# Feed-forward pair combinations on VectorE, early products, and side work moved into the mLSTM stage of a two-layer trunk

## The chip, the cores and the metric

The kernel is one program on one core of a Trainium2 chip. The metric is the device time of one execution in microseconds (us); the kernel before took 3206.36 us as the median of three runs (3194.96 to 3218.95).

## What is computed

The reference is a trunk of two layers over 1024 tokens of width 1024, in float32. Each layer has a token mixer (RWKV-7 in layer 0, a chunked mLSTM in layer 1) and a SwiGLU feed-forward block, each behind an RMS norm whose scale, shift and gate come from the conditioning vector `c` (`mod`):

```python
mod = c_act @ ada_w[i] + ada_b[i]
sh1, sc1, g1, sh2, sc2, g2 = split(mod, 6)
x = x + g1 * mixer(_rms(x) * (1 + sc1) + sh1)      # _rwkv7_mix (i = 0) or _mlstm_mix (i = 1)
x = x + g2 * _swiglu(_rms(x) * (1 + sc2) + sh2, w_gu, w_down)
...
def _swiglu(x, w_gu, w_down):
    gu = x @ w_gu
    return (silu(gu[..., :D_FF]) * gu[..., D_FF:]) @ w_down      # D_FF = 2816
```

After layer 1 a last RMS norm is scaled by `final_w`.

## The kernel before

Activations lie transposed: 8 tiles of 128 features by 512 tokens for each of two token halves (`x[0]`, `x[1]`). A float32 product is made of three reduced-precision ones: `split` (L210) makes a rounded part `hi` on ScalarE and the rest `lo = raw - hi` on VectorE, and for every 128x128 block of weights TensorE runs hi*hi, hi*lo and lo*hi, each a matmul of 128x512.

The feed-forward (`ffn`, L1053) uses a Winograd form of Strassen's scheme over both token halves: instead of 8 block products of half size, `seven` (L902) runs 7 for a pair of output tiles n and n+11, from seven combinations of weight blocks (`wpair`, L863) and seven of activations (`X`). A block product is 4 blocks x 3 = 12 matmuls, so a call of `seven` is 84. There are 11 pairs, each with a call for the gate and one for the up projection. The first two pairs (`NPLAIN`) are done without the scheme: `plain`, 48 matmuls for each of two tiles and two halves, 192 for a pair instead of 168. `wpair` loads two weight tiles, and makes the four sums and differences on GpSimd (L881 to L888, into `ws`), between splits of 512 columns. `keep` stores each pair's results and their own combinations to DRAM (`gd`), and `down` (L987) reads them back for the second matrix, again in seven products, with combinations of its weights that `sums` (L966) wrote to DRAM before (`wsd`).

`sums` and `ada` (layer 1's `mod`, L289) are background work: generators in `self.bg`, of which `wpair` advances `rate` steps each time. A step of `sums` loads four tiles of 128x352, makes four sums on GpSimd and stores four; there are 16 for each layer. `ada` loads 512-column tiles and accumulates on VectorE; a 1-column matmul ends each. In layer 0 the rate is 7, with `sums(0)` and then all six parts of `ada`; in layer 1 it is 1, with `sums(1)`. The mLSTM stage has no background work.

All these transfers are issued by SP's queue, in order: an issue that waits for a buffer holds up those behind it. A scheduler lays the instructions of each engine in one fixed order, and `ahead(...)` raises the priority of some. Buffers are pools by tag (`FROOM` for the feed-forward: 4 `tmp`, 8 `tt`, 3 `wraw`; 8 `x` for activations and later the background).

The RWKV stage (`chunks`, L1386) works through 16 units (8 feature tiles x 2 halves) in a pipeline of preparation, inverse, solve, chain and finish; `fillers` puts dense matmuls between their small, dependent ones, and its last filler is the output projection of token half 0. The projection of half 1 (`second`) comes in `ffn`, after the plain tiles of half 0.

## Time and profile before

| | before |
|---|---|
| median of 3 runs | 3206.36 us (3194.96 to 3218.95) |
| profiled execution, its own time | 3216.39 us |
| span of its trace | 3214.2 us |
| TensorE busy (matmul) | 2946.6 us, 92% |
| VectorE / ScalarE / GpSimd busy | 1950.4 / 1437.8 / 428.8 us |
| granted TensorE clock, mean | 0.905 |

The stages, by what TensorE's matmuls read: layer 0's inputs and RWKV to about 1120 us, feed-forward of layer 0 to about 1943, mLSTM to about 2380, projection and feed-forward of layer 1 to the end. A granted clock of 1.00 is 2.4 GHz, 0.50 is 1.2 GHz. Matmuls overlap their neighbours in the pipeline, so the count of matmuls in a stretch tells more than the duration of one.

### The profile page before, as it was taken

The page shows a single profiled execution, that of the slowest core. Times are in us where ns is not written, and L with a number is a line of the kernel's source. Part 1 is how long each engine was busy: PE and PEld are TensorE (multiplying, and loading weights), DVE is VectorE, ACT ScalarE, POOL GpSimd, SP SyncE. Part 2 cuts the span into 40 slices and gives each one's busy share as a digit, 9 for nine tenths or more (in the row PEclk, how much of TensorE's full clock was granted, in tenths as well). Part 3 has the DMA queues.
Part 4 walks back from the last instruction along what each step waited for, and adds up shares of the span by engine and source line. Part 5 has one row for each costly group of instructions (what it writes and reads, how often), then busy time and mean ns, then how long its engine had stood idle before and what let it go on. Part 6 is the DMA issues. An engine that isn't in the chain of part 4 may idle for free. (4 is left out here: it accounts for less than half of the span.)

```text
span 3214.2 us, 46353 instructions
## 1 busy us (share of the span) xinstructions
PE 2946.6 (92%) x16960; PEld 2318.8 (72%) x16960; DVE 1950.4 (61%) x3736; ACT 1437.8 (45%) x2815; POOL 428.8 (13%) x369
## 2 busy tenths in 40 slices
PE   6899999999999888958899999999988898899997
PEld 5577667777776676747788887777767776688886
DVE  7867576777665447638957656434455564555763
ACT  5656665655654444312335436333334432333551
POOL 0000000000000001652220000000000066431000
PEclk9899688899788598978999999898988899999998
DMA  8764343344533243666737643111144256533852
GB/s 290 266 214 126 94 129 98 104 113 132 152 111 107 66 140 108 207 226 214 236 122 252 215 165 108 33 40 40 46 164 136 97 180 213 184 105 129 288 170 89
DMA packets 318679, 474.78 MB, mean 148 GB/s; under 512 B 120652, under 2 KB 163276, under 8 KB 318452
## 3 DMA queue, kind: packets, MB, share of 16 engines
q1 hardware_dynamic: 304628, 446.66, 43.7%
q10 hardware_dynamic: 13824, 25.17, 2.1%
q8 instruction: 133, 2.18, 0.3%
q14 instruction: 94, 0.77, 0.1%
HBM read 347.98 MB, written 123.73 MB: 147 GB/s over the span
## 5 line engine op out<-in xcount | busy, mean ns | idle before, releaser
L208 PE MATMUL c<-ga,wq 128*128 128x512 f32 x1998 | 490.3, 400 | 53.2 <-ACT tmp L911 32.5
L212 ACT ACTIVATE wq<-wraw 128x512 fp32r<-128x512 f32 (+2 forms) x368 | 248.3, 678 | 584.1 <-PE c L208 265.4
L208 PEld LDWEIGHTS c<-ga,wq 128*128 128x128 f32 x1998 | 382.5, 193 | 142.6 <-ACT tmp L911 37.3
L213 DVE TENSOR_TENSOR wq<-wraw,wq 128x512 fp32r<-128x512 f32 (+2 forms) x368 | 304.6, 833 | 283.7 <-ACT wq L212 280.0
L208 PE MATMUL dn<-a,whi 128*128 128x512 f32 (+2 forms) x1048 | 401.9, 449 | 17.4 <-ACT a L212 6.2
L208 PEld LDWEIGHTS dn<-a,whi 128*128 128x128 f32 (+2 forms) x1048 | 206.1, 204 | 77.9 <-issue 11.5
L208 PE MATMUL c<-gb,wq 128*128 128x512 f32 x1014 | 248.0, 398 | 4.5 <-DVE tt L926 2.3
L208 PE MATMUL dn<-a,wlo 128*128 128x512 f32 (+2 forms) x552 | 244.0, 446 | 7.1 <-ACT tmp L416 2.2
L208 PE MATMUL dn<-ga,wq 128*128 128x512 f32 x894 | 224.3, 400 | 14.9 <-ACT ga L212 11.1
L208 PEld LDWEIGHTS c<-gb,wq 128*128 128x128 f32 x1014 | 192.9, 192 | 49.1 <-DVE tt L926 3.9
L208 PEld LDWEIGHTS dn<-ga,wq 128*128 128x128 f32 x894 | 173.3, 195 | 54.2 <-ACT ga L212 12.1
L213 DVE TENSOR_TENSOR wlo<-wraw,whi 128x1024 fp32r<-128x1024 f32 (+2 forms) x86 | 103.9, 1208 | 142.3 <-ACT whi L212 137.2
L212 ACT ACTIVATE wq<-ws 128x512 fp32r<-128x512 f32 x108 | 67.4, 629 | 221.6 <-POOL ws L882 97.1
L208 PE MATMUL px<-ga,wq 128*128 128x512 f32 x552 | 141.1, 411 | 27.1 <-ACT tmp L911 20.0
L208 PE MATMUL iv<-gb,wq 128*128 128x512 f32 x630 | 151.4, 390 | 0.0
L213 DVE TENSOR_TENSOR wq<-ws,wq 128x512 fp32r<-128x512 f32 x108 | 84.3, 782 | 105.4 <-ACT wq L212 104.5
L208 PEld LDWEIGHTS px<-ga,wq 128*128 128x128 f32 x552 | 109.5, 200 | 53.0 <-ACT tmp L911 21.8
L208 PE MATMUL dn<-gb,wq 128*128 128x512 f32 x522 | 127.9, 398 | 17.9 <-ACT gb L212 10.0
L208 PEld LDWEIGHTS dn<-a,wlo 128*128 128x128 f32 (+2 forms) x552 | 113.9, 207 | 35.9 <-issue 5.7
L212 ACT ACTIVATE whi<-wraw 128x1024 fp32r<-128x1024 f32 (+2 forms) x86 | 89.7, 1044 | 105.8 <-PE dn L208 91.5
L208 PEld LDWEIGHTS iv<-gb,wq 128*128 128x128 f32 x630 | 118.2, 188 | 24.5
L208 PEld LDWEIGHTS dn<-gb,wq 128*128 128x128 f32 x522 | 99.5, 191 | 41.2 <-ACT gb L212 10.3
(547 smaller groups left out, 5562.7 us busy)
## 6 DMA issues: line engine op xcount, KB each, us to landing
wraw<-in_wgu SPq DMA_DIRECT2D x104, 512.0 KB, 3.7
tt<-gd SPq DMA_DIRECT2D x154, 256.0 KB, 4.7
x<-in_ada SPq DMA_DIRECT2D x96, 256.0 KB, 3.8
gd<-tt SPq DMA_DIRECT2D x88, 256.0 KB, 3.1
x<-in_wdn SPq DMA_DIRECT2D x128, 176.0 KB, 3.3
wsd<-x SPq DMA_DIRECT2D x128, 176.0 KB, 1.8
KT<-in_ada SPq DMA_DIRECT2D x40, 512.0 KB, 5.7
gd<-tmp SPq DMA_DIRECT2D x66, 256.0 KB, 3.7
```

The source lines that it names most:

```text
L208: return self.nc.tensor.matmul(out, lhsT, rhs, start=start, stop=stop, **kw)
L212: self.nc.scalar.activation(hi, src, AF.Copy)
L213: self.nc.vector.tensor_tensor(lo, src, hi.bitcast(F32), SUB)
```

## The change

- Weight combinations: `wpair` makes the four sums and differences in place in the two loaded tiles, on VectorE, and splits them in pieces of 1024, 512, 1024 and 1024 columns instead of seven of 512. `down` splits 1024 columns at once as well.
- Pairs: no pair is plain. For eight pairs of layer 0 (0 to 7) and three of layer 1 (0 to 2), `first` runs products 1 and 2 ahead (their operands are blocks of token half 0 alone), stores product 1 to `pd` and the finished first result to `gd`. When their turn comes ("there"), `seven` runs the five other products (60 matmuls) and adds product 1 from `pd` on VectorE, at the two places where ScalarE copied before.
- Where they run: five of layer 0's as the last fillers of the RWKV stage, behind the projection of half 0 and its norm; the other three, and layer 1's three, in `ffn` between the steps that prepare `X`. `second` now comes first in `ffn`. In the loop the pairs with all seven products come first.
- Background: `sums` works on VectorE, in steps of up to 256 columns (24 for a layer), `ada` in tiles of 256 columns; both in one single buffer of four parts (`bgs`, or `st` in the mLSTM stage), so that a step's loads wait until the buffer's last user is done. Layer 0's feed-forward keeps `sums(0)` and three parts of `ada`, at two steps for each `wpair` and one for each weight tile of `down`; the other three parts and `sums(1)` go to the mLSTM stage, at three steps for each weight tile. Layer 1's feed-forward has none.
- The last norm takes the tiles that are finished first ahead of the others.

```diff
-NPLAIN = 2
+EARLY = ((0, 5, 8), (0, 0, 3))
...
-FROOM = {"wraw": (3, 1024), "wq": (8, 1024), "gb": (11, 1024), "ws": (3, 512), "tmp": (4, 512), "ga": (17, 1024),
-         "tt": (8, 512), "rs": (1, 4)}
+FROOM = {"wraw": (3, 1024), "wq": (5, 2048), "w4": (2, 1024), "gb": (11, 1024), "bgs": (1, 1024), "tt": (5, 512),
+         "ga": (17, 1024), "rs": (1, 4)}
...
-    def ada(self, s, w, raw, acc):
...
+    def spare(self):
+
+        return self.t("bgs" if "bgs" in self.pools else "st", [P, 4, 256])
+
+    def ada(self, s):
...
         for f in range(0, D, w):
-            t = self.t(acc, [P, w])
+            room = self.spare()
+            t = room[:, 0]
             for kt in range(KT):
-                m = self.t(self.alt(*raw), [P, w])
+                m = room[:, 1 + kt % 3]
...
-                if kt < KT - 1:
+                if kt % 2 and kt < KT - 1:
                     yield
...
+    def wpair(self, s1, s2, most):
 
...
-        def part(n, src):
-            out[n] = self.two("wq")
-            self.split(*out[n], src)
-        with self.ahead("pair"):
-            r1, r2 = (self.t("wraw", [P, D]) for _ in range(2))
-            nc.sync.dma_start(r1, s1)
-            nc.sync.dma_start(r2, s2)
-            a11, a12, a21, a22 = r1[:, :HT], r1[:, HT:], r2[:, :HT], r2[:, HT:]
-            u, v, w = (self.t("ws") for _ in range(3))
-            add = nc.gpsimd.tensor_tensor
-            part(1, a11)
-            part(2, a12)
-            add(u, a21, a22, ADD)
-            add(v, u, a11, SUB)
-            part(6, v)
-            part(5, u)
-            add(a21, a11, a21, SUB)
-            part(7, a21)
-            part(4, a22)
-            add(w, a12, v, SUB)
-            part(3, w)
+        def parts(ns, src):
+            n = len(ns)
+            q = self.t("wq" if n == 2 else "w4", [P, 2, n * HT], F32R)
+            self.split(q[:, 0], q[:, 1], src)
+            for i, m in enumerate(ns):
+                c = slice(i * HT, i * HT + HT)
+                out[m] = q[:, 0, c], q[:, 1, c]
+        r1, r2 = (self.t("wraw", [P, D]) for _ in range(2))
+        nc.sync.dma_start(r1, s1)
+        nc.sync.dma_start(r2, s2)
+        a11, a12, a21, a22 = r1[:, :HT], r1[:, HT:], r2[:, :HT], r2[:, HT:]
+        if most:
+            parts((1, 2), r1)
+        parts((4,), a22)
+        add = nc.vector.tensor_tensor
+        add(a22, a21, a22, ADD)
+        add(a21, a11, a21, SUB)
+        add(a11, a22, a11, SUB)
+        add(a12, a12, a11, SUB)
+        parts((6, 3), r1)
+        parts((7, 5), r2)
...
-    def seven(self, w, X, tag):
+    def seven(self, w, X, tag, p1=None):
...
-        def copy(ps):
+        def take(ps):
             t = self.t(tag)
-            nc.scalar.activation(t, ps, AF.Copy)
+            if p1 is None:
+                nc.scalar.activation(t, ps, AF.Copy)
+            else:
+                nc.vector.tensor_tensor(t, ps, p1, ADD)
             return t
...
+        c11 = None
+        if p1 is None:
+            self.product(a, w[1], X[1])
+            c11 = take(a)
+            b = other()
+            self.product(b, w[2], X[2])
+            nc.vector.tensor_tensor(c11, b, c11, ADD)
+        self.product(a, w[6], X[6], start=p1 is not None)
+        c12 = take(a)
...
-        c21 = copy(a)
+        c21 = take(a)
...
+    def first(self, l, n, hp, tags):
+
+        nc = self.nc
+        out = []
+        for u in range(2):
+            hi, lo = self.weights(self.A["wgu"][l, NF * u + n])
+            pa, pb = (self.bank("dn") for _ in range(2))
+            self.product(pa, (hi[:, :HT], lo[:, :HT]), hp[:4])
+            p1 = self.t(tags[0])
+            nc.scalar.activation(p1, pa, AF.Copy)
+            nc.sync.dma_start(self.pd[u, n], p1)
+            self.product(pb, (hi[:, HT:], lo[:, HT:]), hp[4:])
+            t = self.t(tags[1])
+            nc.vector.tensor_tensor(t, pb, p1, ADD)
+            out.append(t)
+        g, u = out
+        nc.scalar.activation(g, g, AF.Silu)
+        nc.vector.tensor_tensor(g, u, g, MUL)
+        nc.sync.dma_start(self.gd[0, n], g)
...
-        q = k // 4
-        add = nc.gpsimd.tensor_tensor
+        add = nc.vector.tensor_tensor
         for n in range(4):
-            for c in range(0, k, q):
-                a11, a21, a22, a12 = (self.t("x", [P, q]) for _ in range(4))
+            for c in range(0, k, 256):
+                q = min(256, k - c)
+                room = self.spare()
+                a11, a21, a22, a12 = (room[:, i, :q] for i in range(4))
                 for t, m, o in ((a11, n, 0), (a21, n + 4, 0), (a22, n + 4, k), (a12, n, k)):
                     nc.sync.dma_start(t, w[l, m, :, o + c:o + c + q])
-                s1, s2 = (self.t("x", [P, q]) for _ in range(2))
-                add(s1, a21, a22, ADD)
-                add(s2, s1, a11, SUB)
+                add(a22, a21, a22, ADD)
                 add(a21, a11, a21, SUB)
-                add(a12, a12, s2, SUB)
-                for i, t in enumerate((s1, s2, a21, a12)):
-                    nc.sync.dma_start(self.wsd[i, n, :, c:c + q], t)
+                add(a11, a22, a11, SUB)
+                add(a12, a12, a11, SUB)
+                for i, t in enumerate((a22, a11, a21, a12)):
+                    nc.sync.dma_start(self.wsd[l][i, n, :, c:c + q], t)
                 yield
...
+        _, n0, n1 = EARLY[l]
+        if l == 1:
+            self.store(0, x[0])
+            r = self.rstd(x[0])
+        second()
+        if l == 1:
+            self.norm_blocks(x[0], l, r)
         b11, b21 = self.parts(x[0][:4], "gb"), self.parts(x[0][4:], "gb")
...
+        with self.ahead("norm"):
+            r = self.rstd(x[1])
+        tags = "tt", "tt"
+
+        def some():
+            nonlocal n0
+            if n0 < n1:
+                self.first(l, n0, b11 + b21, tags)
+                n0 += 1
+        some()
+        X = {1: b11, 2: b21}
+        f = [x[0][:4], x[1][:4], x[0][4:], x[1][4:]]
...
+        X[3], X[6] = [], []
         for kt in range(4):
-            f11, f21, f12, f22 = x[0][kt], x[0][kt + 4], x[1][kt], x[1][kt + 4]
-            nc.vector.tensor_tensor(f12, f12, f11, SUB)
-            nc.vector.tensor_tensor(f22, f22, f12, SUB)
-            nc.vector.tensor_tensor(f21, f21, f22, SUB)
...
+            self.norm_blocks(x[1], l, r, (kt, kt + 4))
+            add(f[1][kt], f[1][kt], f[0][kt], SUB)
+            X[3] += self.parts(f[3][kt:kt + 1], "gb" if kt < 3 else "ga")
+            add(f[3][kt], f[3][kt], f[1][kt], SUB)
+            X[6] += self.parts(f[3][kt:kt + 1], "ga")
+        some()
+        X[5] = self.parts(f[1], "ga")
+        X[7] = []
+        for kt in range(4):
+            add(f[0][kt], f[3][kt], f[0][kt], SUB)
+            X[7] += self.parts(f[0][kt:kt + 1], "ga")
+        some()
+        X[4] = []
+        for kt in range(4):
+            add(f[2][kt], f[2][kt], f[3][kt], SUB)
+            X[4] += self.parts(f[2][kt:kt + 1], "ga")
+        while n0 < n1:
+            some()
+        self.rate = rates[0]
+        for n in chain(range(n1, NH), range(n1)):
+            there = n < n1
+            w = wgu[l]
+            p = [None] * 2
+            if there:
+                p = [self.t("tt") for _ in range(2)]
+                nc.sync.dma_start(p[0], self.pd[0, n])
+            sil = self.seven(self.wpair(w[n], w[n + NH], not there), X, "x", p[0])
+            if there:
+                sil[0] = self.t("x")
+                nc.sync.dma_start(sil[0], self.gd[0, n])
+            for t in sil[there:]:
                 nc.scalar.activation(t, t, AF.Silu)
-            up = self.seven(self.wpair(wgu[l, NF + n], wgu[l, NF + n + NH]), X, "tmp")
-            for t, u in zip(sil, up):
+            if there:
+                nc.sync.dma_start(p[1], self.pd[1, n])
+            up = self.seven(self.wpair(w[NF + n], w[NF + n + NH], not there), X, "tt", p[1])
+            for t, u in zip(sil[there:], up[there:]):
                 nc.vector.tensor_tensor(t, u, t, MUL)
-            self.keep(sil, n, up[:3])
-        self.background(1000)
-        self.rate = 0
+            self.keep(sil, n, up[there:][:3], there)
+        self.rate = rates[1]
         x[0] = self.load(self.rooms(0), 0, self.xd[0])
         x[1] = self.load(self.rooms(1), 1, self.xd[1])
         self.down(l, x, done)
+        self.background(1000)
+        self.rate = 0
...
-        r = self.rstd(xs)
+        r = self.rstd(xs[4:] + xs[:4] if hf else xs)
...
         yield from self.project(self.yd[0], "wro", 0, x0, self.a0, PA)
+        self.store(0, x0)
+        self.norm_blocks(x0, 0, self.rstd(x0))
+        hp = []
+        for x in x0:
+            hi, lo = self.a0()
+            self.split(hi, lo, x)
+            hp.append((hi, lo))
+        for n in range(EARLY[0][0], EARLY[0][1]):
+            self.first(0, n, hp, ("mt", "tmp"))
+            yield 11
...
+        self.deep = True
+
+        def second(y, w, l):
             x[1] = self.load(self.rooms(1), 1, None if l == 0 else self.xd[1])
-            run(self.project(y, w, l, x[1], lambda: self.two("ga"), tag))
-        self.bg = chain(self.sums(0), *(self.ada(s, HT, RAW1, "x") for s in (1, 0, 2, 4, 3, 5)))
-        self.ffn(0, x, lambda: second(self.yd[1], "wro", 0, ("tmp",)), lambda j: self.store(j, x[j]), 7)
+            run(self.project(y, w, l, x[1], lambda: self.two("ga"), ("tt",)))
+        self.bg = chain(self.sums(0), *(self.ada(s) for s in (1, 0, 2)))
+        self.ffn(0, x, lambda: second(self.yd[1], "wro", 0), lambda j: self.store(j, x[j]), (2, 1))
...
         self.deep = True
+        self.bg, self.rate = chain(*(self.ada(s) for s in (4, 3, 5)), self.sums(1)), 3
...
         run(ml)
+        self.background(1000)
+        self.rate = 0
...
+        run(self.project(self.yd[0], "wmo", 1, x[0], lambda: self.two("gb"), ("tt",)))
+        self.ffn(1, x, lambda: second(self.yd[1], "wmo", 1), lambda j: self.final(j, x[j]), (0, 0))
```

TensorE near the end of the RWKV stage, in the last unit's chain; `st` is the state, `AR`, `KT`, `SR` and `VU` are the unit's operands, `a` the split activations of token half 0. Before:

```order
L208 MATMUL c_2071_11335<-VU_11188,KT_10616 128x128
L208 MATMUL c_2070_11332<-VU_11188,SR_10571 64x64 x2
L208 MATMUL c_2072_11342<-st_1580,AR_10559 128x128
L208 MATMUL c_2073_11345<-VU_11188,KT_10616 128x128
L208 MATMUL c_2072_11342<-VU_11188,SR_10571 64x64 x2
L208 MATMUL c_2074_11352<-st_1580,AR_10559 128x128
```

Now:

```order
L207 MATMUL c_2145_11687<-st_1582,AR_10561 128x128
L207 MATMUL dn_11713<-a_10964,whi_11709 128x512
L207 MATMUL dn_11713<-a_10963,wlo_11710 128x512
L207 MATMUL dn_11714<-a_10967,whi_11709 128x512
L207 MATMUL c_2146_11690<-VU_11436,KT_10618 128x128
L207 MATMUL c_2145_11687<-VU_11436,SR_10573 64x64 x2
L207 MATMUL dn_11714<-a_10968,whi_11709 128x512
L207 MATMUL dn_11714<-a_10967,wlo_11710 128x512
L207 MATMUL dn_11714<-a_10971,whi_11709 128x512
L207 MATMUL c_2147_11697<-st_1582,AR_10561 128x128
```

Three matmuls of `first` now stand between each two dependent steps of the chain, and 33 more follow the unit's last transposes, ahead of the projection of half 1.

SP in the mLSTM stage, its queue of transfers; `wraw` are the stage's weights, `st` the background's single buffer. Before:

```order
L226 DMA wraw_18551<-in_wo 128x1024
L226 DMA wraw_18610<-in_wqk 128x1024
L226 DMA wraw_18682<-in_wqk 128x1024
L226 DMA wraw_18882<-in_wo 128x1024
L226 DMA wraw_18957<-in_wvm 128x1024
```

Now, the same five weights:

```order
L226 DMA wraw_18479<-in_wo 128x1024
L302 DMA st_17864<-in_ada 128x256 x2
L226 DMA wraw_18555<-in_wqk 128x1024
L302 DMA st_17925<-in_ada 128x256 x8
L302 DMA st_18026<-in_ada 128x256 x8
L302 DMA st_18087<-in_ada 128x256 x3
L226 DMA wraw_18644<-in_wqk 128x1024
L302 DMA st_18087<-in_ada 128x256 x3
L226 DMA wraw_18860<-in_wo 128x1024
L302 DMA st_18087<-in_ada 128x256 x2
L302 DMA st_18186<-in_ada 128x256 x8
L302 DMA st_18466<-in_ada 128x256 x3
```

Between two weight loads that stood next to each other there are now up to 19 background loads, each of which can wait for the buffer.

VectorE in layer 0's feed-forward loop, in a pair whose products 1 and 2 are there (L917 adds product 1 out of PSUM, L934 to L939 add others, L887 to L890 make combinations, L996 to L999 are background). Now:

```order
L934 TENSOR_TENSOR x_13664<-iv_13637,x_13662 128x512
L996 TENSOR_TENSOR bgs_13592<-bgs_13592 128x256
L997 TENSOR_TENSOR bgs_13592<-bgs_13592 128x256
L998 TENSOR_TENSOR bgs_13592<-bgs_13592 128x256
L937 TENSOR_TENSOR x_13662<-c_2413_13666,x_13662 128x512
L999 TENSOR_TENSOR bgs_13592<-bgs_13592 128x256
L212 TENSOR_TENSOR w_2434_13859<-wraw_13856,w_2434_13859 128x512
L939 TENSOR_TENSOR x_13635<-iv_13637,x_13635 128x512
L887 TENSOR_TENSOR wraw_13856<-wraw_13856 128x512
L888 TENSOR_TENSOR wraw_13856<-wraw_13855,wraw_13856 128x512
L917 TENSOR_TENSOR tt_13755<-c_2422_13742,tt_13577 128x512
```

Combinations and background, which were GpSimd's in the kernel before, stand here between the additions out of PSUM that free TensorE's banks.

## Rows read from the trace of the kernel before

**Rows 1.** The page: span, TensorE, its 40 slices and granted clock, a background load.

```profile
span 3214.2 us, 46353 instructions
...
PE 2946.6 (92%) x16960; PEld 2318.8 (72%) x16960; DVE 1950.4 (61%) x3736; ACT 1437.8 (45%) x2815; POOL 428.8 (13%) x369
...
PE   6899999999999888958899999999988898899997
...
PEclk9899688899788598978999999898988899999998
...
x<-in_ada SPq DMA_DIRECT2D x96, 256.0 KB, 3.8
```

**Rows 2.** Busy time by stretch: length, each engine's busy us (instructions), clock, DMA.

```profile
1031.50:1120.00 88.50, 68.60 (x724) 53.99 (x723) 40.54 (x117) 42.79 (x121) 4.28 (x3) 0.53 0.30 88
1120.00:1142.00 22.00, 10.51 (x38) 8.01 (x39) 11.12 (x22) 15.59 (x41) 1.64 (x1) 0.56 0.05 18
1142.00:1222.00 80.00, 80.00 (x355) 66.26 (x354) 36.35 (x43) 27.85 (x35) 0.00 (x0) 1.00 0.51 169
1222.00:1246.00 24.00, 10.57 (x40) 8.28 (x39) 13.87 (x24) 11.59 (x18) 1.01 (x1) 0.64 0.16 55
...
1300.00:1440.00 140.00, 98.21 (x389) 78.26 (x388) 64.43 (x67) 30.48 (x53) 85.23 (x72) 0.84 0.64 209
1440.00:1620.00 180.00, 159.81 (x673) 128.19 (x674) 159.66 (x221) 51.51 (x88) 50.04 (x32) 0.93 0.71 232
...
1700.00:1948.00 248.00, 244.74 (x1079) 201.57 (x1078) 145.54 (x233) 111.71 (x193) 3.73 (x11) 0.99 0.60 200
...
2026.00:2365.00 339.00, 334.62 (x1772) 260.94 (x1772) 131.12 (x344) 108.05 (x255) 19.82 (x31) 0.91 0.13 43
...
2424.00:2452.00 28.00, 18.10 (x58) 13.81 (x58) 16.77 (x27) 15.77 (x26) 1.01 (x1) 0.70 0.40 123
...
2528.00:2556.00 28.00, 16.48 (x65) 13.20 (x64) 18.98 (x30) 13.30 (x21) 1.96 (x1) 0.70 0.14 47
...
2640.00:2790.00 150.00, 121.16 (x483) 95.40 (x482) 71.53 (x87) 39.99 (x71) 88.21 (x73) 0.92 0.64 211
...
3187.00:3214.00 27.00, 11.00 (x48) 9.10 (x46) 10.81 (x17) 3.44 (x6) 1.01 (x1) 0.69 0.21 78
```

**Rows 3.** Waits of TensorE: for whom, us in total, times, longest.

```profile
PE c L208 <- ACT tmp L911: 32.5, 4, 22.3
```

**Rows 4.** Timeline of SP's queue in layer 0's loop: start us, us, instruction.

```profile
1358.86 1.86 SPq L977 DMA_DIRECT2D x<-in_wdn  x4
...
1364.96 3.14 SPq L984 DMA_DIRECT2D wsd<-x  x4
```

**Rows 5.** Timeline of GpSimd: first sums of the third and the sixteenth step.

```profile
1303.81 1.33 POOL L979 TENSOR_TENSOR x<-x,x 128x352 f32<-128x352 f32 x1 [4.87 <-DMA x<-in_wdn]
...
1431.55 0.93 POOL L979 TENSOR_TENSOR x<-x,x 128x352 f32<-128x352 f32 x1 [5.41 <-DMA gd<-tmp]
```

**Rows 6.** Groups by shape, 1260 to 1700 us: busy us, mean ns, idle before.

```profile
L213 DVE TENSOR_TENSOR wq<-wraw,wq 128x512 fp32r<-128x512 f32 x70 | 65.2, 934 | 44.6 <-ACT wq L212 44.3
...
L881 POOL TENSOR_TENSOR ws<-wraw 128x512 f32<-128x512 f32 x18 | 26.0, 1446 | 177.1 <-DMA wraw<-in_wgu 110.4 <-DVE wq L213 34.7 <-DVE x L303 32.0
```

**Rows 7.** Groups by shape, 1700 to 1960 us, where GpSimd does next to nothing.

```profile
L213 DVE TENSOR_TENSOR wq<-wraw,wq 128x512 fp32r<-128x512 f32 x58 | 39.5, 688 | 43.2 <-ACT wq L212 43.0
...
L1047 DVE SCALAR_TENSOR_TENSOR x<-c,mod,x 128x512 f32<-128x512 f32 x8 | 6.0, 749 | 3.4 <-PE c L208 3.4
...
L213 DVE TENSOR_TENSOR wlo<-wraw,whi 128x1024 fp32r<-128x1024 f32 x2 | 2.4, 1216 | 0.0
...
L929 DVE TENSOR_TENSOR tt<-c,tt 128x512 f32<-128x512 f32 x1 | 0.7, 692 | 2.3 <-PE c L208 2.3
```

**Rows 8.** Groups by shape in the mLSTM stage, 2026 to 2365 us.

```profile
L213 DVE TENSOR_TENSOR wlo<-wraw,whi 128x1024 fp32r<-128x1024 f32 x18 | 22.0, 1224 | 111.8 <-ACT whi L212 107.3 <-PE sc L208 4.5
L1252 DVE SCALAR_TENSOR_TENSOR pt<-iv,gj,br 128x128 f32<-128x128 f32 x32 | 10.4, 345 | 0.3
```

More of the change, by code (lines that the diff above doesn't have):

```diff
@@ L319, in rstd @@
         nc = self.nc
[L320 to L321 removed]
+        acc, mt = ("mt", "mt") if "mt" in self.pools else ("bgs", "tt")
+        acc = self.t(acc)
         nc.scalar.activation(acc, xs[0], AF.Square)
@@ L931, in seven, with keep @@
         nc.vector.tensor_tensor(c12, c, c12, ADD)
-        return c11, c12, c21, c22
-    def keep(self, g, n, room):
+        return [c11, c12, c21, c22]
+    def keep(self, g, n, room, there):
         nc = self.nc
@@ L941, in put @@
             nc.sync.dma_start(self.gd[i - 1, n], t)
-        put(1, g11)
+        if not there:
+            put(1, g11)
         put(2, g21)
@@ L1022, in down, with run @@
             fresh = p in (1, 2, 4, 5)
-            def run(n, units, lo, first, last):
-                for u, w in enumerate(units):
-                    o = lo // P + 4 * u
-                    e = o + 4 if o + 4 <= NH else NH
-                    self.product(ps[n], w, xs[o:e], start=first and u == 0 and fresh, stop=last and u == len(units) - 1)
+            def run(n, w, lo, first, last):
+                self.product(ps[n], w, xs[lo // P:lo // P + w[0].shape[-1] // P], start=first and fresh, stop=last)
             for n in range(4):
@@ L1051, in store, with ffn @@
             self.nc.sync.dma_start(self.xd[j][kt], xs[kt])
[L1053 removed]
+    def ffn(self, l, x, second, done, rates):
         nc = self.nc
         wgu = self.A["wgu"]
[L1057 to L1088 removed]
@@ L1456, in build @@
         self.gd = self.dram.tile([7, NH, P, HT], F32, name="gd")
-        self.wsd = self.dram.tile([4, 4, P, NH * P], F32, name="wsd")
+        self.pd = self.dram.tile([2, NH, P, HT], F32, name="pd")
+        self.wsd = [self.dram.tile([4, 4, P, NH * P], F32, name=f"wsd{l}") for l in range(2)]
         self.phase(ROOM)
@@ L1534, in build @@
         x[0] = self.load(self.rooms(0), 0, self.xd[0])
-        run(self.project(self.yd[0], "wmo", 1, x[0], lambda: self.two("ga"), ("tmp",)))
-        self.bg = self.sums(1)
-        self.ffn(1, x, lambda: second(self.yd[1], "wmo", 1, ("tmp",)), lambda j: self.final(j, x[j]), 1)
+        run(self.project(self.yd[0], "wmo", 1, x[0], lambda: self.two("gb"), ("tt",)))
+        self.ffn(1, x, lambda: second(self.yd[1], "wmo", 1), lambda j: self.final(j, x[j]), (0, 0))
         self.phase()
```

85 lines of the change are left out of this document (18 added, 67 removed).

## The prediction

> **What bounds the kernel now.** I read the page first: TensorE is busy for 92% of the span, and its slices fall below 9 at the start, between about 1040 and 1610 us, between 2330 and 2810, and at the very end; the granted clock is below full speed in most of the same slices [rows 1]. So TensorE sets the end, and what a change is worth is the matmuls it removes, the stalls it closes and the low clock behind them. Next the stretches [rows 2]. Dense work at full clock ran 355 matmuls in 80 us, 0.225 us each. A stretch's deficit is its length less 0.225 us for each of its 128x512 matmuls; it holds the idle time and the lost clock together. In layer 0's feed-forward it is 24 - 40 x 0.225 = 15 us at 1222, 140 - 389 x 0.225 = 52.5 at 1300 to 1440, 180 - 673 x 0.225 = 28.6 at 1440 to 1620, and about 5 in 1700 to 1948. In layer 1's it is 28 - 58 x 0.225 = 15 at 2424, 28 - 65 x 0.225 = 13.4 at 2528, 150 - 483 x 0.225 = 41.3 at 2640 to 2790, and 27 - 48 x 0.225 = 16 at the end. The mLSTM stage is nearly full: 334.6 of 339 us busy. Third, the waits: the longest in the loops, 32.5 us, is TensorE held by ScalarE's copies into `tmp` [rows 3]. Such a copy is short; it is late when `tmp` is not free, because its store to DRAM stands in SP's queue behind background loads and stores. The queue shows it: four background loads are issued by 1360.7, and their stores only at 1365.0, with two results' stores between [rows 4]. From the third to the sixteenth step of `sums` the distance is (1431.55 - 1303.81) / 13 = 9.8 us [rows 5].
>
> **The change, part by part**, as gain (+) or loss (-) against the profiled execution's own 3216.4 us, which lies 10 us above the median of the three runs.
>
> A. Matmuls. A plain pair of 192 becomes one of 168, twice in each layer: 96 fewer, 96 x 0.225 = **+22**. Nothing replaces them.
>
> B. Five `first` in the end of the RWKV stage: 5 x 48 = 240 matmuls, 54 us of dense work, leave the feed-forward. The end of that stage, 1031.5 to 1120, has TensorE busy 68.6 of 88.5 us at clock 0.53 [rows 2]: small dependent matmuls. With dense ones between them the clock should stay high. The old work then takes between 68.6 x 0.53 = 36 us and an unchanged 69, and the old waits stay to between 0 and 20 us, so the stretch takes from 54 + 36 = 90 to 54 + 69 + 20 = 143 us. I take 105, nearer the low end, since the row's clock is almost at its lower level throughout. The 22 us behind it, of which half is idle, shrink to about 5, since 33 matmuls of the last `first` cover the last unit's store and reload. Old 88.5 + 22 = 110.5, new 110; but the 38 matmuls (8.5 us) that ran in the 22 us are still to be done: 54 - 8.5 = **+45** (bounds +8 to +61). The extra norm and splits on VectorE and ScalarE lie beside the chain.
>
> C. The stall at 1222 (norm of half 1, then `X`) gets three `first` as cover, 32 us of TensorE. But VectorE has to make `X` in that time, about 50 operations of 0.69 us (35 us) and the `first`'s own splits, and the last seven products' operands come at its pace; I leave 10 of 15: **+5** (0 to +15).
>
> D. Layer 0's loop, deficit 81. GpSimd's sums leave, and VectorE's 512-column operations fall from 0.934 us, their mean beside GpSimd [rows 6], to 0.688 [rows 7]. 1024 columns take 1.216, an operand out of PSUM 0.692; so 256 columns are 0.42 [rows 7], and an `ada` operation of 256 lies between 0.345 and 0.749, about 0.48 [rows 7, 8]. A `wpair` and `seven` with all products then need VectorE for 3 x 1.22 + 0.69 + 4 x 0.69 + 4 x 0.69 + half of 8 x 0.69 = 12.6 us, against 84 x 0.225 = 18.9 of TensorE: no bound. In a pair that is "there" they need 2 x 1.22 + 0.69 + 4 x 0.69 + 5 x 0.69 + half of 7 x 0.69 = 11.7 us against 60 x 0.225 = 13.5. Sixteen such calls are 187 us, and the background in them, 12 steps of `sums` (4 x 0.42) and 20 of `ada` (2 x 0.48), adds 39: 226 us of VectorE against 216 of TensorE. VectorE becomes the bound there. From 1440 to 1620 it was busy 159.66 of 180 us, 89%, while TensorE starved [rows 2]; at that share 226 us take 255. So 39 us of deficit remain: **+42** (bounds 0 to +78).
>
> E. Layer 1: `second` now covers the stall at 2424, and three `first` part of that at 2528; of 28.4 us I leave 10, as in C. The loop has no background and only six calls with products "there", 11.7 of 13.5 us; of 41.3 I leave 3. **+56** (+35 to +65).
>
> F. The last norm: four squares and additions of 0.69 us come before the last product instead of behind it: **+3**.
>
> G. The mLSTM stage takes 24 steps of `sums` and 12 `ada` quarters of 8 loads through three slots. A quarter is about three rounds of 3.8 us to land [rows 1] and one operation, 13 us; with 9.8 a step SP's chain is 24 x 9.8 + 12 x 13 = 391 us. The room for it, from layer 0's last product (30 us before 1943) to 2380, is 467 us, so it fits with a sixth to spare, but not everywhere: up to 19 loads stand between two weights. VectorE has room for the work (131 of 339 us busy, rows 2), but its order is fixed too: it waits 107 us in this stage for rounded weights [rows 8], and a background sum behind such a wait holds SP. Bounds: 0, if the weights' buffers cover it all, and 24 x 3.75 = 90 us, if a step costs what it cost at 1300 to 1440 (52.5 us for 14 steps). I take **-15**, near the low end, because at 2026 to 2365 the transfers kept the DMA engines 13% busy against 64% at 1300.
>
> H. Layer 0's `down` now carries seven quarters of `ada` in SP's queue, 91 us of the 248 in which it must also bring the results and weights. These are asked for long ahead: **-4** (0 to -20).
>
> Sum: 22 + 45 + 5 + 42 + 56 + 3 - 15 - 4 = +154, and 3216 - 154 = **3062 us**.
>
> On D one rule speaks against the change. The Trainium skill, in Perfetto Trace Analysis, section Optimizing Scalar/DVE Operations, says that GpSimd and VectorE share a read port into SBUF, so that moving work between the two might not help. The rows show a dearer operation on GpSimd (1.446 us for what VectorE does in 0.688, rows 6, 7) and a loss of 0.246 us on VectorE beside it, far less than one GpSimd operation. By the rule VectorE would be as loaded as both were, and D and the loop part of E would be nothing.
>
> **The rivals.**
>
> 1. The loops keep their deficits (D and the 38 of E are 0), because additions out of PSUM now stand behind combinations and background on VectorE: 3062 + 42 + 38 = 3142. For it: 226 against 216 us in D, and `tt` with five buffers of which a pair takes all. Against: layer 1's loop has no background left, and VectorE was busy 71.5 of 150 us there. The rule above ends here too. 8%.
>
> 2. The mLSTM stage pays 90 us instead of 15: 3062 + 75 = 3137. For: the order of SP, the single buffer. Against: weights are requested two or more ahead. 7%. With rival 1 together, 3217: 4%.
>
> 3. Slower: the single buffer makes every one of the 48 steps of `sums` cost 3.75 us of TensorE, and each `ada` quarter 28.6 / 12 = 2.4 (1440 to 1620 held the `ada` of twelve half rows). Layer 0's steps then cost 90 instead of 39 (+51), the mLSTM's 90 instead of 15 (+75), and 24 quarters 57: 3062 + 183 = 3245. It decides from the point at which SP's chain in the mLSTM stage is longer than its 467 us, that is above about 13 us for a step. Against: VectorE's sums take 1.7 us where GpSimd's took 4. 5%.
>
> 4. The RWKV end is held up: `first` lengthens the dependent steps by as much as it brings, B is 0, 3107. 4%.
>
> 5. Better: VectorE hides behind TensorE after all and the background costs nothing: D at 78, G at 0, 3011. 15%.
>
> That the change does not do what it says is excluded for A, which is a count in the order of instructions.
>
> **The numbers.** The forecast, 3062, has 57%; alone it reaches from 3025 to 3100. The range takes in case 5, the bounds of B and rivals 1 and 2: 2995 to 3145. About 1% of 3206, 32 us, is what a measurement of this kernel tells from no change: faster means below 3174. Adding the cases, and moving some of rivals 1 and 2 up for their spread, gives faster 0.87, the same 0.08, slower 0.05.
>
> **What would show it.** A: 96 fewer 128x512 matmuls. B: a clock near 1 and dense matmuls from about 1040 to 1120, and no gap before the projection of half 1. C, E: no stretch under 0.8 of the clock at the two norms. D: in the last two thirds of layer 0's loop VectorE at 85 to 90% and TensorE's waits ended by it, at the additions of product 1; with little VectorE there and SP's issues waiting, it is rival 3. G: a mLSTM stage of 435 to 460 us with waits on weights or on VectorE. I am wrong if layer 0's loop starves on weights, or if the mLSTM stage grows by more than 40 us.

## The result, and the profile after

The changed kernel takes 3091.4 us (median of four, 3080.0 to 3093.3) beside 3209.3 us for the kernel before: a ratio of 0.963, 95% interval 0.959 to 0.967. The forecast, 3062 us, was made against a profiled execution of 3216.4 us; the profiled one of the changed kernel took 3080.0, so 136 us were gained there of the 154 forecast. It was the fastest of its four executions; by the medians the gain is 118. The sum was nearly right, but its terms were not.

The page of the changed kernel, the rows that answer to [rows 1]; the last is a background load.

```profile
span 3078.2 us, 46320 instructions
...
PE 2890.2 (94%) x16864; PEld 2265.4 (74%) x16864; DVE 2068.1 (67%) x4128; ACT 1394.3 (45%) x2629; POOL 73.9 (2%) x97
...
PE   6799989999999899999998988999989999999998
...
PEclk9898688999968799999999999988989999999998
...
bgs<-in_ada SPq DMA_DIRECT2D x96, 128.0 KB, 3.0
```

TensorE has 96 matmuls fewer, and 56 us less of work. VectorE has taken GpSimd's work and is at 67%. Of the dips of before those of the loops are gone; the end of the RWKV stage still shows one at low clock, and new weak ones stand between 1600 and 1930 us.

Busy time by stretch of the changed kernel, in the columns of [rows 2]: the end of the RWKV stage (three rows), the norm of half 1, layer 0's loop (three, and its calls with products there), `down`, the mLSTM stage, the two norms of layer 1, its loop, the end.

```profile
1019.00:1045.00 26.00, 22.24 (x116) 17.56 (x115) 14.94 (x35) 9.73 (x19) 2.04 (x1) 0.55 0.43 113
1045.00:1062.00 17.00, 13.54 (x249) 11.26 (x248) 10.14 (x27) 12.16 (x28) 0.00 (x0) 0.50 0.01 2
1062.00:1155.00 93.00, 88.08 (x691) 68.44 (x689) 48.25 (x115) 52.56 (x140) 4.91 (x3) 0.98 0.38 119
...
1240.00:1262.00 22.00, 18.07 (x69) 13.52 (x68) 20.60 (x34) 9.06 (x13) 0.00 (x0) 0.92 0.44 143
1300.00:1440.00 140.00, 136.82 (x593) 109.87 (x592) 110.82 (x185) 39.05 (x53) 0.00 (x0) 1.00 0.70 226
1440.00:1540.00 100.00, 94.65 (x404) 74.73 (x403) 86.63 (x153) 23.55 (x30) 0.00 (x0) 0.98 0.68 218
1540.00:1605.00 65.00, 62.64 (x276) 50.71 (x275) 54.76 (x87) 16.87 (x23) 0.00 (x0) 1.00 0.72 241
...
1378.00:1603.00 225.00, 216.05 (x930) 171.73 (x928) 192.32 (x324) 55.07 (x70) 0.00 (x0) 0.99 0.71 232
...
1605.00:1849.00 244.00, 222.45 (x957) 180.23 (x956) 147.47 (x243) 94.03 (x142) 3.48 (x11) 0.96 0.68 218
1849.00:2305.00 456.00, 424.59 (x2266) 330.92 (x2264) 281.70 (x688) 162.97 (x349) 25.56 (x38) 0.92 0.43 136
2340.00:2362.00 22.00, 17.60 (x77) 14.45 (x76) 9.55 (x13) 6.93 (x10) 1.01 (x1) 0.87 0.52 184
2440.00:2460.00 20.00, 16.63 (x64) 12.74 (x63) 15.69 (x23) 8.77 (x13) 0.00 (x0) 0.91 0.19 70
2640.00:2840.00 200.00, 200.00 (x878) 163.56 (x877) 135.29 (x190) 61.85 (x83) 0.00 (x0) 1.00 0.43 149
3055.00:3078.00 23.00, 10.95 (x51) 8.93 (x49) 8.40 (x13) 1.26 (x2) 1.01 (x1) 0.74 0.25 92
```

Layer 1's loop has no idle time in the row shown; layer 0's has a deficit of 6.6 + 9.1 + 2.9 = 18.6 us where it had 81, and in its calls with products there VectorE is busy for 192 of 225 us. `down` of layer 0 starves, some 244 us for 924 matmuls that need 208.

Since executions drift by up to 28 us before the first place that the change touches, the kernels are compared by stages, cut at the same matmuls in each timeline. "Tail": from the last matmul of the projection of half 0 in the RWKV stage to the first that reads a weight of the feed-forward's pool. "To down": from there to `down`, whose 924 matmuls are counted back from its last one. "mLSTM": up to the first matmul of layer 1's projection. The last two columns are the rest, cut at `down` of layer 1.

| us, from the profiled execution | tail | to `down` | `down` 0 | mLSTM | layer 1 to `down` | `down` 1 and end |
|---|---|---|---|---|---|---|
| before | 111 | 596 | 212 | 439 | 598 | 235 |
| changed | 141 | 443 | 247 | 456 | 531 | 241 |
| changed, repeated (e13) | 141 | 440 | 250 | 468 | 529 | 242 |
| before, additions on VectorE (e5) | 111 | 524 | 213 | 444 | 567 | 235 |
| changed, additions on GpSimd (e1) | 141 | 539 | 244 | 491 | 593 | 242 |
| eight firsts in the feed-forward (e2) | 128 | 499 | 250 | 468 | 531 | 242 |
| `ada` in the loop (e3) | 148 | 473 | 248 | 478 | 530 | 244 |
| side work back (e4) | 141 | 466 | 279 | 443 | 534 | 243 |
| norm ahead (e9) | 141 | 445 | 247 | 474 | 530 | 240 |
| side work laid elsewhere (e10) | 141 | 442 | 246 | 471 | 538 | 246 |
| stores last (e11) | 144 | 443 | 250 | 469 | 529 | 242 |
| weights of `down` in halves (e12) | 148 | 446 | 233 | 467 | 529 | 238 |
| e12 without mLSTM side work (e14) | 141 | 443 | 232 | 444 | 531 | 241 |
| e12 without firsts in layer 1 (e15) | 141 | 442 | 232 | 471 | 535 | 237 |

### The profile page after: what moved, and what is told of

Same layout as the page of the kernel before. It is cut to its first block, busy times and chain, and to the rows that moved or that the text cites. A ratio compares the mean times of both kernels' runs of the same rounds, so it can differ in the third digit from the quotient of the medians.

```text
span 3078.2 us, 46320 instructions
## 1 busy us (share of the span) xinstructions
PE 2890.2 (94%) x16864; PEld 2265.4 (74%) x16864; DVE 2068.1 (67%) x4128; ACT 1394.3 (45%) x2629; POOL 73.9 (2%) x97
## 4 chain that ended last, share of the span: by engine, by line
PE 66%; DVE 12%; DMA 10%; issue 5%; ACT 4%; SPq 1%; POOL 1%; DVEq 0%; POOLq 0%; ACTq 0%
PE dn L207 24%; PE c L207 19%; PE iv L207 9%; PE px L207 6%; PE sc L207 5%; DMA wraw<-wsd 2%; DMA bgs<-in_ada 1%; DMA tt<-gd 1%; DMA bgs<-in_wdn 1%; DVE wq L212 1%; DMA wraw<-in_wdn 1%; PE tr L207 1%; ACT wq L211 1%; DMA wsd<-bgs 1%; DVE ga L212 1%
## 5 line engine op out<-in xcount | busy, mean ns | idle before, releaser
L207 PE MATMUL dn<-a,whi 128*128 128x512 f32 (+1 forms) x1224 | 458.7, 439 | 16.9 <-ACT a L211 5.5
L211 ACT ACTIVATE wq<-wraw 128x1024 fp32r<-128x1024 f32 x202 | 210.6, 1057 | 364.7 <-DVE wraw L890 121.6
L207 PE MATMUL c<-ga,wq 128*128 128x512 f32 x1446 | 356.6, 395 | 11.7 <-ACT ga L211 6.9
L207 PEld LDWEIGHTS c<-ga,wq 128*128 128x128 f32 x1446 | 270.6, 189 | 79.6 <-ACT ga L211 9.4
L212 DVE TENSOR_TENSOR wq<-wraw,wq 128x1024 fp32r<-128x1024 f32 x202 | 244.5, 1220 | 123.8 <-ACT wq L211 123.6
L207 PEld LDWEIGHTS dn<-a,whi 128*128 128x128 f32 (+1 forms) x1224 | 235.3, 200 | 86.4 <-issue 14.4
L207 PE MATMUL iv<-ga,wq 128*128 128x512 f32 x552 | 136.1, 389 | 0.0
L207 PEld LDWEIGHTS iv<-ga,wq 128*128 128x128 f32 x552 | 103.6, 188 | 21.6
L207 PE MATMUL c<-ga,w 128*128 128x512 f32 x372 | 97.7, 406 | 9.1 <-ACT w L211 5.0
L793 DVE SCALAR_TENSOR_TENSOR st<-st,dl,c 64x64 f32<-64x64 f32 x256 | 71.2, 278 | 44.8 <-PE c L207 40.3
```

The source lines that it names most:

```text
L207: return self.nc.tensor.matmul(out, lhsT, rhs, start=start, stop=stop, **kw)
L211: self.nc.scalar.activation(hi, src, AF.Copy)
L212: self.nc.vector.tensor_tensor(lo, src, hi.bitcast(F32), SUB)
L793: nc.vector.scalar_tensor_tensor(st[hs, hs], st[hs, hs], dl[hs, c:c + 1], p3[hs, hs], MUL, ADD)
```

## The experiments

**Which engine adds (e1, e5).** Two kernels, each with the other's engine:

```diff
e1, from the changed kernel, in wpair and in sums
-        add = nc.vector.tensor_tensor
+        add = nc.gpsimd.tensor_tensor
e5, from the kernel before, in wpair and in sums
-        add = nc.gpsimd.tensor_tensor
+        add = nc.vector.tensor_tensor
```

> The changed kernel with the additions of weight blocks (in the pairs and in the background sums) on GpSimd again, everything else as changed. My theory, from D: an addition of 512 columns takes 1.4 us there instead of 0.7, and VectorE's splits beside it about a quarter of a microsecond more for each 512 columns, so the loops lose again: layer 0's loop 20 to 50 us, layer 1's 5 to 20, in all about 3091 + 45 = 3136 us (3110 to 3165). Rival, the shared port: moving work between the two engines changes nothing, 3080 to 3100. Second rival: in the calls with products already there VectorE was the bound, and freeing it of four additions gains, 3070 to 3085.

> The kernel before with one part of the change alone: the additions of weight blocks, in the pairs and in the background sums, on VectorE, still into tiles of their own and with splits of 512 columns. If the engine is what mattered in D and E (in the changed kernel the additions on GpSimd cost 189 us), layer 1's loop loses most of its deficit of 41 us and layer 0's 81 falls by some 20: 3210 - 55 = 3155 us (3130 to 3185). If it was the layout around it (additions in place behind each other, fewer wide buffers) that makes GpSimd dear in the changed kernel alone, the kernel before gains little: 3195 to 3215.

Measured: e1 3280 us, 1.022 of the kernel before (1.017 to 1.028): 189 us above the changed kernel, four times what I expected, and 2% slower than before. e5 3110 us, 0.970 (0.967 to 0.973): in the kernel before, the engine alone brings 100 us, where the whole change brings 118; I had expected 55. Groups by shape of e1 in layer 0's feed-forward, in the columns of [rows 6], first GpSimd and then VectorE, this one also with the least, median and greatest duration of its eleven, and the longest wait of ScalarE:

```profile
L889 POOL TENSOR_TENSOR wraw<-wraw,wraw 128x512 f32<-128x512 f32 x22 | 31.6, 1434 | 1.5
...
L954 DVE TENSOR_TENSOR x<-x,x 128x512 f32<-128x512 f32 x11 | 16.7, 1521 | 0.3
...
L954 DVE TENSOR_TENSOR x<-x,x x11: 683/1660/1666, 1306.8 to 1689.3; 128x512 f32<-128x512 f32 x11
...
ACT wq L211 <- POOL wraw L890: 141.8, 22, 14.0
```

The same two in the changed kernel's loop, and two background operations:

```profile
L890 DVE TENSOR_TENSOR wraw<-wraw 128x512 f32<-128x512 f32 x21 | 14.4, 688 | 0.4
...
L954 DVE TENSOR_TENSOR x<-x,x 128x512 f32<-128x512 f32 x10 | 6.8, 682 | 0.0
...
L307 DVE SCALAR_TENSOR_TENSOR bgs<-bgs,ca 128x256 f32<-128x256 f32 x36 | 17.2, 479 | 3.1 <-DMA bgs<-in_ada 2.9
...
L996 DVE TENSOR_TENSOR bgs<-bgs 128x256 f32<-128x256 f32 x18 | 7.6, 421 | 10.1 <-DMA bgs<-in_wdn 7.3 <-issue 2.3 <-DMA gd<-x 0.3
```

On GpSimd an addition takes twice as long, and four stand behind each other (5.7 us) before two of a pair's wide splits may start; ScalarE waits 142 us for the last of them. Of VectorE's own additions beside them, which read and write SBUF, one group takes 1.52 us instead of 0.68 in the mean of eleven: 1.66 us in the median, and 0.68 where GpSimd stands idle beside it. It is the group that is hit hardest. That the layout of the change (in place, one behind the other) is what makes GpSimd so dear there fits these waits, but no run has the layout alone. In e5, TensorE no longer waits for ScalarE's copies into `tmp`: the longest waits of TensorE from 1230 us to `down`, where [rows 3] had 22.3 us, are

```profile
PE c L208 <- ACT ga L212: 9.2, 1, 9.2
PE dn L208 <- DVE tmp L926: 6.2, 4, 2.9
```

and a step of `sums` follows the last after 7.7 us (first sums at 1277.16 and, 15 steps on, 1393.23) instead of 9.8, by which the stores behind it in SP's queue can leave sooner.

**Early products in the tail (e2, e9).**

```diff
e2 (and without the splits that nobody reads then)
-EARLY = ((0, 5, 8), (0, 0, 3))
+EARLY = ((0, 0, 8), (0, 0, 3))
e9, in fillers
-        self.norm_blocks(x0, 0, self.rstd(x0))
-        hp = [] ...
+        with self.ahead("norm"):
+            self.norm_blocks(x0, 0, self.rstd(x0))
+            hp = [] ...
```

> The changed kernel with no early products in the end of the RWKV stage: all eight of layer 0 run in its feed-forward. Measured by stage marks, B brought about 24 us and not the 45 forecast. If that reading is right the kernel takes 3091 + 24 = 3115 us, and the end of the RWKV stage runs at half clock again without them. If B was worth its forecast and something else ate it, 3136. If the early products only lengthened the chain they stand in, 3091 or less.

> The changed kernel with the norm of half 0 and the splits behind it given a higher priority in the scheduler, so that the early products can enter the end of the RWKV stage sooner. In the changed kernel its first 40 us still run at half clock, since the first early product comes only 27 us behind the projection. If that delay is what keeps the stage long, the tail of 141 us loses 10 to 20: about 3078 us (3068 to 3088). If the chain of the last unit sets the pace there, the norm only delays it: 3091 or more (3088 to 3105).

Measured: e2 3142 us, 0.977 (0.972 to 0.983), 51 above the changed kernel; by stages 13 less in the tail and 56 more behind it, 43. e9 3087 us, 0.964 (0.961 to 0.968): no difference. The tail of e2, and of e9 in three parts and in its two pieces at half clock:

```profile
1030.00:1140.00 110.00, 86.75 (x796) 67.39 (x796) 47.39 (x137) 49.53 (x133) 4.28 (x3) 0.51 0.24 68
```

```profile
1002.00:1028.00 26.00, 18.86 (x229) 15.29 (x230) 20.56 (x45) 18.06 (x39) 1.01 (x1) 0.68 0.51 134
1028.00:1060.00 32.00, 31.47 (x253) 24.30 (x253) 21.75 (x66) 21.58 (x55) 1.64 (x1) 0.94 0.25 72
1060.00:1143.00 83.00, 75.83 (x568) 58.49 (x566) 32.69 (x72) 37.96 (x102) 3.27 (x2) 0.82 0.36 120
...
1011.50:1032.00 20.50, 17.02 (x201) 13.29 (x199) 15.20 (x31) 16.46 (x33) 0.00 (x0) 0.50 0.48 133
1066.00:1093.00 27.00, 27.00 (x241) 21.07 (x235) 7.82 (x18) 12.35 (x34) 0.00 (x0) 0.50 0.16 50
```

The changed kernel's one piece at half clock, and the same 240 matmuls of the tail in the changed kernel and in e12:

```profile
1022.00:1066.00 44.00, 38.42 (x377) 31.11 (x377) 24.43 (x61) 22.20 (x51) 2.04 (x1) 0.50 0.26 66
```

```profile
1093.70:1109.10 15.40, 15.31 (x250) 12.02 (x246) 6.35 (x14) 10.52 (x31) 0.00 (x0) 1.00 0.34 104
```

```profile
1082.90:1104.80 21.90, 21.90 (x247) 16.86 (x242) 6.36 (x14) 10.55 (x29) 0.00 (x0) 0.62 0.24 74
```

Without early products the tail is at half clock nearly throughout; with them 54 us of dense work cost 13. In e9 the early products enter sooner (36 of their matmuls stand in the first 44 us of the tail, 4 in the changed kernel) and the clock is up after 30 us instead of 48, but it falls again for 27 us: 47.5 us at half clock against 44 in the changed kernel, and the tail takes the same 141 us. So e9 doesn't tell whether the clock or the last units' chain sets the length. The table holds a better test. In e3 and e12 the tail has the same matmuls in the same order as in the changed kernel and is 6.5 us longer, 148 us. The clock was at half for 17 us more there, and the 6.5 us are lost in that place, 21.9 us for what takes 15.4 at full clock; none of it is regained behind. There the clock counts. Why it fell in these two executions stays open; e14 and e15, which have e12's edit, take 141 us. That the tail without early products is 128 us where the kernel before had 111 goes with the norm of half 0, which the change moved into it.

**Side work (e3, e4, e10, e14, e13).**

```diff
e3
-        ... lambda j: self.store(j, x[j]), (2, 1))
+        ... lambda j: self.store(j, x[j]), (4, 0))
e4 (layer 0: ada 1, 0, 2, 4, 3, 5, rates (4, 1); mLSTM: none; layer 1: sums(1), rates (2, 0))
e10 (layer 0: ada 1, 0, rates (2, 1); mLSTM: ada 2, 4, 3, 5, rate 3; layer 1: sums(1), rates (2, 0))
e14, on e12 (and layer 0's results in place of those left out)
-        self.bg, self.rate = chain(*(self.ada(s) for s in (4, 3, 5)), self.sums(1)), 3
+        self.bg, self.rate = iter(()), 0
```

> The changed kernel with four background steps for each pair in layer 0's loop and none in its down: sums(0) and the three parts of ada end within the loop. My theory of the loss in down (244 us against 212 before): the background loads in SP's queue stand ahead of weights and results, so without them down takes 215 to 225 us and the loop, with twice the steps in a call, loses 10 to 20: about 3083 us (3068 to 3098). Rival: down loses by its fewer and wider buffers and by the stores of half 0 in the queue; it stays at 240 or more, the loop still loses 10 to 20, 3105 us.

> The changed kernel with the mLSTM stage free of background again: the three parts of ada go back to layer 0's feed-forward (four steps a pair, one a weight of down) and sums(1) to layer 1's loop (two steps a pair). My theory: the mLSTM stage gives back the 17 us by which it grew (456 to 439), layer 0's loop and down lose 20 to 40 and layer 1's loop about 10, together 3091 - 17 + 40 = 3114 us (3095 to 3135). Rival, a step costs the same wherever it stands: 3085 to 3095. Rival, the mLSTM stage is the dear place: below 3080.

> The changed kernel with the side work laid elsewhere: sums(1) in layer 1's loop (two steps a pair, where they cost 4 us in the last study), the gate part of ada in the mLSTM stage instead of layer 0's feed-forward. Layer 0's feed-forward then carries 24 sums and 8 quarters of ada, the mLSTM stage 16 quarters and no sums. My theory: layer 0's down and loop gain 6 to 12, the mLSTM stage 5 to 12, layer 1's loop loses 4: about 3079 us (3068 to 3089). Rival, a step costs the same wherever it stands: 3091.

> The version with down's weights in halves (median 3067 us), without any background in the mLSTM stage: three parts of the conditioning of layer 1 and its combined weights of down are left out and layer 0's are used for them. It prices term G as a whole. The stage took 439 to 444 us in three kernels without this work and 467 to 478 in six with it, so I expect 442 there and 3067 - 27 = 3040 us (3030 to 3050). If the first profile of the changed kernel was right (456 us), 3067 - 14 = 3053 us. If the longer stage has another reason (other buffers, the order at its start), 3067.

> The changed kernel itself, once more, beside the run above: a second profile and five more times. Its median should lie within 10 us of 3091; the mLSTM stage, which took 456 us in its first profile and 468 to 478 in four other kernels that do not touch it, shows which of these is typical. Where the mLSTM stage is at 465 or more, G was nearer -28 than the -17 of the first profile.

Measured: e3 3136 us, 0.977 (0.970 to 0.983); e4 3127, 0.975 (0.971 to 0.979); e10 3101, 0.967 (0.964 to 0.970); e14 3055, 0.952 (0.949 to 0.956), 12 below e12; e13 3090, 0.962 (0.959 to 0.965). e3 refutes my theory of `down`: with no `ada` in it `down` still takes 248 us, of which TensorE waits 10.5 at its start for the last of the loop's `ada`, and the loop pays 30 for two more steps a pair. TensorE's waits for `ada` in e3, from 1250 us up to the end of that one:

```profile
PE tr L207 <- DVE bgs L307: 23.6, 8, 10.5
```

e4 lies in its range, but its parts were off: layer 0's loop and `down` lost 55 us, not 20 to 40, and layer 1's loop 3, not 10. e10 shows no gain: the mLSTM stage stays at 471 us with other and fewer transfers (16 quarters of `ada`, no `sums`), and layer 1's loop pays 7. The mLSTM stage with side work, e13, and without, e14, in the columns of [rows 2]:

```profile
1845.60:2314.20 468.60, 433.29 (x2265) 336.80 (x2263) 282.18 (x688) 163.66 (x349) 25.61 (x38) 0.90 0.42 133
```

```profile
1843.40:2287.70 444.30, 421.03 (x2217) 329.43 (x2215) 212.58 (x490) 165.65 (x351) 24.66 (x38) 0.91 0.19 62
```

All kernels without the work took 439 to 444 us there, those with it 456 and 467 to 478 (e1 491). The work thus costs 12 us by the medians of e12 and e14, whose intervals overlap, and some 24 by stages. Which of its operations cost that stays open; in the changed kernel TensorE is idle for 8.0 us in one place, before `VU` some 40 us into the stage, and for 2.2 right behind.

**Stores and weights of `down` (e11, e12).**

```diff
e11, in down
-            if p == 4:
+            if p == 4 and l == 1:
                 done(0)
+        if l == 0:
+            done(0)
         done(1)
e12, in down, three places
-                run(n, weights(p, n, 0, D), 0, True, False)
-                    run(n, weights(p, n, D, k), D, False, True)
+                run(n, weights(p, n, 0, 768), 0, True, False)
+                    run(n, weights(p, n, 768, k), 768, False, True)
```

> The changed kernel, but layer 0's down stores half 0 of the residual at its end, together with half 1, and not between the weights of its last products. In layer 0's down TensorE stood 8.3 us at the norm of half 0 (ScalarE was waiting for weights of the last products, 6 us each) and the clock fell behind it. If the stores, each of which waits in SP's queue for its sum, are what delays those weights, down falls from 247 us by 10 to 15: about 3079 us (3072 to 3086). If the weights are late for another reason, 3091 (3086 to 3100).

> The changed kernel with the weights of down cut into 768 and 640 columns instead of 1024 and 384, in both layers; both pieces then use the five wide buffers and none the two narrow ones. In the changed kernel's down ScalarE waits 77 us for weights from DRAM (9 us in the kernel before): its split of a narrow piece stands until TensorE frees one of two narrow buffers, the next wide piece is asked for only then and comes 4 to 6 us late, and the squares of the norm stand behind it. If that is what down loses (35 us in layer 0, 8 in layer 1, against the kernel before), it gives back 10 to 20 us in layer 0 and some in layer 1: 3091 - 18 = 3073 us (3062 to 3084). If the buffers are not the reason, 3091 (3084 to 3105).

Measured: e11 3095 us, 0.966 (0.963 to 0.969): no difference, and no test either: in SP's timeline the stores stand at the same places as in the changed kernel, and those between the last weights are half 1's in both, against what I expected. e12 3067 us, 0.956 (0.951 to 0.960) beside 3090 for the changed kernel: the fastest version that computes everything. ScalarE's waits in layer 0's `down`, before, changed, and in e12:

```profile
ACT wq L212 <- PE c L208: 36.2, 22, 2.2
...
ACT wq L212 <- DMA wraw<-wsd: 9.1, 5, 3.8
...
ACT ga L212 <- DMA tt<-gd: 6.1, 6, 2.1
...
ACT wq L212 <- DMA wraw<-in_wdn: 3.5, 2, 2.9
```

```profile
ACT wq L211 <- DMA wraw<-wsd: 54.5, 14, 6.4
ACT ga L211 <- DMA tt<-gd: 19.7, 16, 3.7
ACT wq L211 <- DMA wraw<-in_wdn: 18.7, 7, 5.9
ACT w L211 <- PE c L207: 16.3, 6, 4.4
```

```profile
ACT wq L211 <- PE px L207: 25.7, 9, 4.6
ACT wq L211 <- PE c L207: 23.6, 11, 3.2
ACT ga L211 <- DMA tt<-gd: 18.6, 18, 2.5
ACT wq L211 <- DMA wraw<-in_wdn: 11.4, 7, 3.6
...
ACT wq L211 <- DMA wraw<-wsd: 10.0, 11, 2.3
```

The changed kernel cuts 1408 columns into 1024 and 384. The narrow piece goes to `w4`, which has two buffers; ScalarE's split waits for TensorE to free one, and the next wide weight, whose buffer is released only by the splits, comes late. In halves of 768 and 640 both go to the five wide buffers. ScalarE then waits for TensorE, as before, and for weights from DRAM 21 us instead of 73 (13 in the kernel before). Its waits for the loop's results (`gd`) ahead of `ga` stay, 18.6 us after 19.7, where the kernel before had 6.1; `tt`, into which these are loaded, went from eight buffers to five, but no run tests that. In the three kernels with this cut (e12, e14, e15) `down` takes 232 to 233 us in layer 0, 14 to 18 less than in the two profiles of the changed kernel; in layer 1 it takes 237 to 241, 0 to 5 less.

**Early products in layer 1 (e15).**

```diff
on e12
-EARLY = ((0, 5, 8), (0, 0, 3))
+EARLY = ((0, 5, 8), (0, 0, 0))
```

> The version with down's weights in halves, without early products in layer 1: its eleven pairs are all done whole, the same number of matmuls in all. E forecast that three early products cover part of the stall at the norm of half 1 (28 us of it and the stall before, 10 left); if so this kernel loses 10 to 18 us: 3067 + 14 = 3081 us (3074 to 3088), in layer 1's part between the mLSTM stage and down (532 us). If the loop's gain is the engine's alone and VectorE's preparation sets the pace behind the norm anyway, 3067 (3062 to 3073).

Measured: 3075 us, 0.957 (0.954 to 0.961), and 535 us in its stage instead of 529 (e12) and 531 (e14): they are worth 4 to 6 us by the stage, 8 by medians whose intervals overlap.

## Why the sum was right and its terms were not

The stage table splits the 136 us, rounded, with 0.225 us for a dense matmul as in the prediction. That the sum came within 18 us of the forecast is luck: B, F and H fell 61 us short, and C and D together brought 41 more than forecast.

| step | forecast | measured | how |
|---|---|---|---|
| A | 22 | 22 | 96 matmuls fewer |
| B | 45 | 24 | 111 to 141, of which 54 are dense work taken from later |
| C, D | 47 | 88 | 596 - 443 - 54 - 11 of A |
| E | 56 | 56 | 598 - 531 - 11 of A |
| F | 3 | -6 | 235 to 241 |
| G | -15 | -17 | 439 to 456 |
| H | -4 | -35 | 212 to 247 |
| ahead of all this | 0 | 5 | drift between executions |

- **B** failed at "The extra norm and splits on VectorE and ScalarE lie beside the chain". The norm at least lies in it: e2's tail, which has the norm but neither the splits nor the products, is 17 us longer than that of the kernel before. Its other half held late: the dense work entered from 1045 us on, the clock rose at 1066 and not at 1040. What that delay cost stays open, since e9 has as much time at half clock. Rival 4 is refuted, the early products bring 43 to 51 us against none.
- **C and D** were undersized. C went from 15 to 22 - 69 x 0.225 = 6.5, where 10 were left by the forecast. D failed at "226 us of VectorE": its mechanism was right, its size was not. The count was right: the sixteen calls' operations add up to 187 us by their measured durations, and the background in the row from 1378 to 1603 to 37. But these durations overlap. VectorE in that row, two places:

```profile
1400.83 0.68 DVE L917 TENSOR_TENSOR x<-px,tt 128x512 f32<-128x512 f32 x1
1401.43 0.68 DVE L889 TENSOR_TENSOR wraw<-wraw,wraw 128x512 f32<-128x512 f32 x1
...
1412.34 0.69 DVE L888 TENSOR_TENSOR wraw<-wraw,wraw 128x512 f32<-128x512 f32 x1
1413.06 0.69 DVE L889 TENSOR_TENSOR wraw<-wraw,wraw 128x512 f32<-128x512 f32 x1
```

Operations that need nothing of one another start 0.60 us apart and last 0.68; those behind each other in the same two loaded tiles start 0.72 apart. The durations of the row's 324 operations add up to 212 us, and VectorE was busy for 192. The 89% of the forecast is such a busy share. With 226 x 192 / 212 = 205 us at that share the calls take 230 us against 216 of TensorE, 14 lost instead of 39; TensorE lost 225 - 930 x 0.225 = 16. The sign for D came out: VectorE at 85%, and TensorE's longest waits in the loop for the additions of product 1 (L917, 4.9 us). Besides, 72 one-column matmuls of `ada` were counted as whole ones in the deficit of before, which was therefore up to 16 us larger than 81. e5 shows the cause of most of it: moving the additions alone takes 72 us from this stage. The other 16 of the 88 no run divides, between the early products, the wider splits and the `ada` that left. Rival 1 is refuted; rival 5 was nearly right in D and wrong in G. By the forecast's reading of the shared read port (the Trainium skill, Perfetto Trace Analysis, Optimizing Scalar/DVE Operations) D would have been nothing; e1 and e5 differ from their partners by 189 and 100 us. The port's cost may still be what is seen in e1, 1.52 us for 0.68 beside GpSimd, and it speaks for the move.
- **E** came out at its size, with another split than I gave: 31 us are what the engine alone brings (e5, 598 to 567). The two stalls of layer 1 fell from 28.4 to 4.7 + 5.6 us as forecast, but e15 does without the three early products and loses 4 to 8. The order of `second` and the preparation in pieces are left as the reason for most; no run tests them alone.
- **F** had the right end (from 16 to 23 - 51 x 0.225 = 11.5) but the stage is 6 us longer, so `down` of layer 1 is some 10 slower, which the forecast left out. That the reason is layer 0's isn't shown: the three kernels with e12's cut give back 0 to 5.
- **G** held by its stage, 456 us as said. Other executions put it nearer -28 (e13 at 468 us), still within 0 to -90. Rival 2 (-90) is refuted, rival 3 too: no stage pays what it asked for.
- **H** is the step whose mechanism failed: "These are asked for long ahead". They are not: SP's load of a weight waits for a buffer that a split has to read first, and that split waits behind the one that stands for `w4`. The forecast went by the queue and not by the two buffers of `w4`, which stand in the diff. Of the 35 us, the cut of e12 gives back 14 to 18; `ada` explains about 10 (e3, 237 us without the wait at its start); the rest is open.

## What to carry to other kernels

Move elementwise work off GpSimd one edit at a time and time that edit alone: here it brought 100 us where the whole change brought 118, and the changed kernel with its additions on GpSimd was slower than the old one. When a pool is split into wide and narrow buffers, count how many pieces ahead the smallest pool lets the engine run that fills it in order; everything behind that piece in the engine's order waits with it. Cutting pieces evenly over one pool can be worth more than the widest instruction. When you ask whether an engine will be the bound, add up the distances between starts, not the durations: in the calls above the durations of VectorE's operations are 10% too much.
